# Input projection of a hybrid decoder layer: the weight's hi part times both parts of normed x in one 512-column product, halves summed afterwards

## The chip, the cores and the metric

The kernel runs on one core of a Trainium2 chip. The metric is the device time of one execution in microseconds; lower is better. Each time is the median of repeated executions.

## The reference, cut to what matters

One layer of a decoder with 256 tokens (SEQ), 1024 channels (D_MODEL), float32 throughout:

```python
h = rmsnorm(x, norm_mix)
proj = h @ w_in                                # 1024 x 9488, split into the pieces below
m_z, m_xbc, m_dt, b_qkv, c_qkv, c_f, d_q, d_kv, gate_logits = split(proj)
y_a = mamba2_branch(m_z, m_xbc, m_dt, ...)     # conv of 4 taps, SSD scan, silu(z) gate
y_b = moba_attention(bq, bk, bv, rel_bias)     # with 256 tokens: plain causal attention with bias
y_c = forgetting_attention(cq, ck, cv, c_f)    # bias from a cumulative log forget gate
y_d = sliding_window_attention(dq, dk, dv, sinks, rel_bias)
branch_out = einsum('bsiw,iwd->bsid', stack([y_a, y_b, y_c, y_d]), w_branch)
x = x + sum(sigmoid(gates) * branch_out) @ w_out
h = rmsnorm(x, norm_ffn)
x = x + (silu(h @ w_gate) * (h @ w_up)) @ w_down
out = rmsnorm(x, norm_final)
```

## The kernel before

**Split products.** Every weight and every activation that goes into a large product is cut into a hi part (rounded to the matmul's format fp32r by a copy on ACT) and a lo part (the difference, by DVE). A product is then hi times hi, hi times lo and lo times hi, all added in PSUM. `xx(k)` holds both parts of x for the k-th block of 128 channels as [128, 2, 256]: x times its norm weight, but not yet times the row factor `r1` (the reciprocal root of the mean square), which is applied after the product.

**Weights.** Weights come from HBM in pieces of 1 MB, one after the other in the order of `stream()`: first the projection pieces of `FIRST`, then for each branch its gate pieces and its `wb` pieces, then `wo`, 22 `gu` pieces and 11 `dn` pieces. `fetch` (L333 to L339) issues the load on SP's queue into one of 3 `raw` buffers, `split_hi` (L347) makes the hi part on ACT and `split_lo` (L355) the lo part on DVE, in two halves of 1024 columns each. When the second lo half of a piece is written, the load of the piece three places on is issued.

**Projection pieces.** A transposed piece (all of `xbc`, `z`, `qk` and `qD`; 256 weight columns, the weight is the stationary operand) is computed by `tr_groups` (L493) in two groups j, one for each 128 columns. Both groups share one PSUM bank of the tag `acc` (3 banks). A group of `two` and `mm` is: for each of 8 blocks k the hi weight times x hi (L264) and the hi weight times x lo (L265), 256 columns each, then 8 times the lo weight times x hi (L262). That makes 24 matmuls of 256 columns. A `v` piece and a gate piece (L1044) are natural: x is stationary, the weight moves, 12 matmuls of 512 columns in a group.

**After a product.** One DVE operation over both groups takes the bank out and applies the row factor, broadcast over partitions in `rb` (L936 for q and k, L630 for the convolution's input, L661 for z). `end_v` (L944) and `end_gate` (L968) do it on ACT with a scale for each token.

**Order of the work.** Everything is emitted in one program order; each engine takes its instructions in that order. Between PE's groups the `Weaver` emits the other work. It keeps a planned clock for PE, DVE and ACT. `tick`, called after each group with a cost of 2620 ns (`GROUP`), first runs one step of every urgent task (the ends of products, added by `add`), then lets `split_ahead` cut further weights, then runs steps of the other tasks, each only if DVE's and ACT's planned clocks stay within `SLACK` (3500 ns) of PE's and the buffers it names are free. Buffers are counted by tag: `acc` 3 (PSUM banks), `w2` 6, `w1` 4. `until` runs tasks until given flags are set, whatever the clocks say; `until_free` does the same when a new bank is wanted and none is free.

**The beginning.** x comes transposed with the first weights (`hd`, 8 loads); then `raw_n0`, x again in natural order (`xn`, for the mean square), `raw_qkB0`, small constants, `raw_vB0`, masks and `raw_vB1` follow on SP's queue. PE computes xbc0, n0, a transposed row of `r1` (L477), qkB0, vB0 and vB1, then xbc2 and the other pieces of `FIRST`. The steps of `conv` (SSD's input convolution of xbc0 and xbc1, 2 `w2` buffers each) and `softplus_cums` (a long chain on POOL that gives `dt` and the cumulative sums) run beside them.

**The feed-forward part** already has the form that the change brings: from the fifth `gu` piece on (`wide`, L267, with `normed_x2`, L1157) the hi weight times [x hi | x lo] is one matmul of 512 columns (L273), followed by the lo weight times x hi with 256 columns (L277), and `end_ffn` adds the halves (L1180 on ACT, L1181 on DVE).

**The end.** For each half t of the tokens the last `dn` products are added to the residual (L1265), squared and summed (L1268 on ACT, L1276 on DVE), the reciprocal root is taken on POOL (L1279), the first 512 channels are multiplied by the norm weight (L1280) and scaled on ACT (L1282), the other 512 on DVE (L1283), and the output is stored. In the second half the last 128 channels have a bank of their own, `pd_end`, finished last.

## Time and profile before

| what | value |
|---|---|
| median of 3 runs | 511.25 us (510.37 to 513.1) |
| profiled execution, whole time | 511.43 us |
| profiled execution, span from first to last instruction | 509.7 us |
| mean granted TensorE clock | 0.998 of full speed |
| instructions | 7927 |

The span is what the rows below are measured in, from its start; 1.73 us of the profiled execution lie around it. Busy time of an engine is the time in which it executes; a matmul's own duration is longer than the distance to the next one, since matmuls overlap, so distances between starts are read for PE.

### The profile page before, as it was taken

What the parts mean: (1) busy time and instruction counts of PE and PEld (TensorE: products, weight loads), DVE (VectorE), ACT (ScalarE), POOL (GpSimd) and SP (SyncE); (2) the same over time, 40 slices, a digit from 0 to 9 for tenths busy, and PEclk for the clock granted to TensorE, in tenths of its full rate; (3) what the DMA queues carried; (4) which work ended last, traced back from release to release, by engine and by line L of the source; (5) the groups of instructions that cost most, each with busy time, mean ns of one, the idle gap of its engine ahead of it and who ended that gap; (6) DMA issues with size and microseconds to landing.
All of it is one profiled execution on the core that took longest, in us unless ns stands there. A gap on an engine that the chain in (4) does not pass through costs nothing.

```text
span 509.7 us, 7927 instructions
## 1 busy us (share of the span) xinstructions
PE 501.6 (98%) x3106; PEld 443.5 (87%) x3106; DVE 352.2 (69%) x654; ACT 285.6 (56%) x507; POOL 31.4 (6%) x58
## 2 busy tenths in 40 slices
PE   8999999999999999999999999999999999999994
PEld 8988999979988878788888899998888888888884
DVE  5597689697884969496393676688767767754425
ACT  6687356557465747645535435776556656734322
POOL 0008110011220100000000000000000000000001
PEclk9999999999999999999999999999999999999999
DMA  8964546545455464247266391536456455676202
GB/s 306 386 258 176 201 151 213 211 181 180 167 195 178 131 242 157 114 143 271 82 239 256 101 345 59 196 143 233 166 187 222 168 174 210 237 267 228 84 0 82
DMA packets 16161, 96.06 MB, mean 188 GB/s; under 512 B 1979, under 2 KB 2651, under 8 KB 5884
## 3 DMA queue, kind: packets, MB, share of 16 engines
q1 hardware_dynamic: 14844, 91.36, 49.6%
q0 software_dynamic: 1280, 4.20, 2.7%
q8 instruction: 24, 0.39, 0.3%
q14 instruction: 13, 0.11, 0.1%
HBM read 94.46 MB, written 1.09 MB: 187 GB/s over the span
## 4 chain that ended last, share of the span: by engine, by line
PE 96%; issue 1%; DMA 1%; DVE 0%; ACT 0%; POOLq 0%; POOL 0%; SPq 0%
PE pg L1044 17%; PE gu L273 13%; PE pd L1238 11%; PE pb L262 9%; PE gu L277 7%; PE pvC L1044 2%; PE pvB L1044 2%; PE xbc L451 2%; PE qkC L264 2%; PE qkB L262 2%; PE po L262 2%; PE gu L262 2%; PE qkC L262 2%; PE gu L265 2%; PE qkB L265 2%; PE qkC L265 2%
## 5 line engine op out<-in xcount | busy, mean ns | idle before, releaser
L273 PE MATMUL gu<-x3x,hi_gu 128*128 128x512 f32 x288 | 68.7, 391 | 0.0
L1044 PE MATMUL pg<-hi_g,xx 128*128 128x512 f32 x256 | 64.4, 393 | 0.0
L273 PEld LDWEIGHTS gu<-x3x,hi_gu 128*128 128x128 f32 x288 | 52.9, 188 | 10.3
L355 DVE TENSOR_TENSOR lo_gu<-raw_gu,hi_gu 128x1024 fp32r<-128x1024 f32 x44 | 53.3, 1222 | 6.2 <-ACT hi_gu L347 6.2
L1044 PEld LDWEIGHTS pg<-hi_g,xx 128*128 128x128 f32 x256 | 47.4, 188 | 11.0 <-issue 1.5
L1238 PE MATMUL pd<-hi_dn,aa 128*128 128x512 f32 (+1 forms) x176 | 46.6, 387 | 0.0
L347 ACT ACTIVATE hi_g<-raw_g 128x1024 fp32r<-128x1024 f32 x32 | 32.9, 1053 | 23.8 <-DMA raw_g<-in_w_dram 11.0
L347 ACT ACTIVATE hi_gu<-raw_gu 128x1024 fp32r<-128x1024 f32 x44 | 44.0, 1048 | 1.6 <-PE gu L265 1.6
L355 DVE TENSOR_TENSOR lo_dn<-raw_dn,hi_dn 128x1024 fp32r<-128x1024 f32 x22 | 26.1, 1221 | 21.9 <-ACT hi_dn L347 21.8
L355 DVE TENSOR_TENSOR lo_g<-raw_g,hi_g 128x1024 fp32r<-128x1024 f32 x32 | 38.7, 1234 | 2.7 <-ACT hi_g L347 2.7
L1238 PEld LDWEIGHTS pd<-hi_dn,aa 128*128 128x128 f32 x176 | 32.9, 188 | 6.6
L277 PEld LDWEIGHTS gu<-x3x,lo_gu 128*128 128x128 f32 x288 | 36.9, 191 | 1.4
L277 PE MATMUL gu<-x3x,lo_gu 128*128 128x256 f32 x288 | 37.4, 283 | 0.0
L347 ACT ACTIVATE hi_dn<-raw_dn 128x1024 fp32r<-128x1024 f32 x22 | 22.2, 1051 | 25.2 <-PE pd L1238 25.2
L1044 PE MATMUL pg<-lo_g,xx 128*128 128x512 f32 x128 | 34.2, 389 | 0.0
L1181 DVE TENSOR_TENSOR gs<-gu,ge 128x256 f32<-128x256 f32 x36 | 15.2, 424 | 20.0 <-ACT ge L1180 20.0
L1044 PEld LDWEIGHTS pg<-lo_g,xx 128*128 128x128 f32 x128 | 24.0, 188 | 5.0
L1180 ACT ACTIVATE ge<-gu 128x256 f32<-128x256 f32 x36 | 13.8, 383 | 25.5 <-PE gu L277 25.5
L1238 PE MATMUL pd<-lo_dn,aa 128*128 128x512 f32 (+1 forms) x88 | 26.9, 387 | 0.0
L355 DVE TENSOR_TENSOR lo_wb<-raw_wb,hi_wb 128x1024 fp32r<-128x1024 f32 x16 | 19.4, 1220 | 7.4 <-ACT hi_wb L347 7.4
L968 ACT ACTIVATE gate<-pg,r1h 128x512 f32<-128x512 f32 x16 | 11.0, 688 | 19.9 <-PE pg L1044 19.8
L347 ACT ACTIVATE hi_wb<-raw_wb 128x1024 fp32r<-128x1024 f32 x16 | 16.7, 1055 | 7.3 <-PE pg L1044 7.3
(322 smaller groups left out, 1115.7 us busy)
## 6 DMA issues: line engine op xcount, KB each, us to landing
raw_gu<-in_w_dram SPq DMA_DIRECT2D x22, 1024.0 KB, 4.9
raw_g<-in_w_dram SPq DMA_DIRECT2D x16, 1024.0 KB, 4.9
raw_dn<-in_w_dram SPq DMA_DIRECT2D x11, 1024.0 KB, 4.8
raw_wb<-in_w_dram SPq DMA_DIRECT2D x8, 1024.0 KB, 5.3
raw_qkB<-in_w_dram SPq DMA_DIRECT2D x4, 1024.0 KB, 4.9
raw_qkC<-in_w_dram SPq DMA_DIRECT2D x4, 1024.0 KB, 4.8
raw_wo<-in_w_dram SPq DMA_DIRECT2D x4, 1024.0 KB, 4.8
hd<-in_head_dram SPq DMA_DIRECT2D x7, 384.0 KB, 7.1
```

Of the source, the lines that this page charges most:

```text
L262: pe.matmul(o, l, r, start=start, stop=stop)
L264: pe.matmul(o, l, r[:, 0, :], start=start, stop=False)
L265: pe.matmul(o, l, r[:, 1, :], start=False, stop=stop)
L273: pe.matmul(b, wh(k), x(k), start=i == 0, stop=False)
L277: pe.matmul(b[:, 0, :], wl(k), x(k)[:, 0, :], start=False, stop=i == n - 1)
L347: act.activation(parts[name][0][:, s], raws[name][:, s], AF.Copy)
L355: dve.tensor_tensor(lo[:, s], raws[name][:, s], hi[:, s].bitcast(F32), ALU.subtract)
L968: act.activation(gates[b, t][:, 512 * nh : 512 * nh + 512], p, AF.Tanh, scale=r1h[:, t : t + 1])
L1044: pe.matmul(pg[t], l, r, start=kh == 0 and i == 0, stop=kh == 1 and i == len(terms) - 1)
L1180: act.activation(e[:, j, :], p[j][:, 1, :], AF.Copy)
L1181: dve.tensor_tensor(s[:, j, :], p[j][:, 0, :], e[:, j, :], ALU.add)
L1238: pe.matmul(o, l, r, start=start and j == 0, stop=stop and j == len(terms) - 1)
```

## The change

The pieces from xbc2 on that are not `v` pieces (`WIDE`, 13 pieces of two groups) are computed from a normed x. After the row factor is known, eight tasks `normed_x` make `xr(k)`: x (loaded once more, transposed, as `xTa`) times norm weight times row factor on DVE, a copy to the hi part on ACT, the difference to the lo part on DVE. The stream waits for all eight before xbc2. Each group of a `WIDE` piece has its own bank: 8 matmuls of the hi weight times [x hi | x lo], 512 columns wide, then 8 of the lo weight times x hi into the first 256 columns. `halves` takes the second half of the bank out on ACT and adds it to the first on DVE; for q and for z a constant factor is applied there. The natural pieces after xbc2 (vC and all gates) use `xr` as well, so that their ends scale by a constant. At the end of the kernel the multiplication by the final norm weight moves from the last step of each token half to its first, and the residual addition of the bank whose last 128 columns end later is cut in two.

```diff
--- before.py
+++ after.py
@@ -26,6 +26,11 @@
 
 
 FIRST = ("xbc0 n0 qkB0 vB0 vB1 xbc2 qkB1 xbc3 z0 qkB2 z1 qkB3 qD0 qkC0 vC0 vC1 qkC1 qD1 qkC2 qkC3").split()
+NORMED = FIRST[FIRST.index("xbc2") :]
+WIDE = [n for n in NORMED if n[0] != "v"]
 
 
 
@@ -476,6 +481,35 @@
         for t in range(2):
             pe.transpose(p[:, t, :], r[:, t : t + 1].broadcast_to([128, 128]), ident)
         return flat(p)
+    xa = [slot("xTa%d" % i) for i in range(2)]
+    for i in range(2):
+        nc.sync.dma_start(xa[i], A["xT"][:, 4 * i : 4 * i + 4, :])
+    xr = []
+    def normed_x(k):
+        yield Need(dve=400, act=310, w1=1)
+        if not xr:
+            xr.append(parts_of([slot("xr%d" % i, (128, 2, 2, 256), F32R) for i in range(4)]))
+        u = work("xu%d" % k, [128, 256], "w1")
+        dve.scalar_tensor_tensor(u, xa[k // 4][:, k % 4, :], nm_mix[:, k : k + 1], rb[:, 1, :], ALU.mult, ALU.mult)
+        h_, l_ = (xr[0](k)[:, i, :] for i in range(2))
+        act.activation(h_, u, AF.Copy)
+        yield Need(dve=340)
+        dve.tensor_tensor(l_, u, h_.bitcast(F32), ALU.subtract)
+        rel(w1=1)
+        wv.done.add("xr%d" % k)
+    def halves(o, p, f=1.0):
+        e = work("he", [128, 256], "w1")
+        act.activation(e, p[:, 1, :], AF.Copy, scale=f)
+        if f == 1.0:
+            dve.tensor_tensor(o, p[:, 0, :], e, ALU.add)
+        else:
+            dve.scalar_tensor_tensor(o, p[:, 0, :], f, e, ALU.mult, ALU.add)
+        rel(acc=1, w1=1)
 
 
     def nat_groups(name, hi, lo, n=256):
@@ -623,13 +657,22 @@
 
     def conv(i, p):
 
-        yield Need(dve=650, w2=2)
-        u = work("cu%d" % i, [128, 2, 259], "w2")
-        dve.memset(u[:, :, 0:3], 0.0)
         if i > 1:
-            dve.tensor_tensor(u[:, :, 3:259], p, rb2(1), ALU.mult)
-            rel(acc=1)
+            yield Need(dve=340, act=310, w2=2, w1=1)
+            hold(w2=1)
+            u = work("cu%d" % i, [128, 2, 259], "w2")
+            dve.memset(u[:, :, 0:3], 0.0)
+            for j in range(2):
+                if j:
+                    yield Need(dve=340, act=310, w1=1)
+                while len(p) <= j:
+                    yield Need()
+                halves(u[:, j, 3:259], p[j])
+            rel(w2=1)
         else:
+            yield Need(dve=650, w2=2)
+            u = work("cu%d" % i, [128, 2, 259], "w2")
+            dve.memset(u[:, :, 0:3], 0.0)
             for j in range(2):
                 dve.tensor_tensor(u[:, j, 3:259], p[j], rb[:, 1, :], ALU.mult)
             rel(**{("att", "acc")[i]: 2})
@@ -656,10 +699,17 @@
         wv.done.add("xbc%d" % i)
 
     def silu_z(i, p):
-        yield Need(dve=600, act=520, w2=2)
+        yield Need(dve=340, act=310, w2=2, w1=1)
+        hold(w2=1)
         zh = work("zh%d" % i, [128, 2, 256], "w2")
-        dve.tensor_tensor(zh, p, rb2(2), ALU.mult)
-        rel(acc=1)
+        for j in range(2):
+            if j:
+                yield Need(dve=340, act=310, w1=1)
+            while len(p) <= j:
+                yield Need()
+            halves(zh[:, j, :], p[j], 0.5)
+        rel(w2=1)
+        yield Need(dve=600, act=520, w2=1)
         th = work("zt%d" % i, [128, 2, 256], "w2")
         act.activation(th, zh, AF.Tanh)
         yield Need(dve=600)
@@ -931,6 +981,14 @@
         wv.later(lambda js=js: fox_quad(js), ["qkC%d" % j for j in js] + ["vC0", "vC1", "cum"], True)
 
 
+    def end_halves(name, o, p, fs):
+        for j in range(2):
+            yield Need(dve=340, act=310, w1=1)
+            while len(p) <= j:
+                yield Need(w1=1)
+            halves(o[:, j, :], p[j], fs[j])
+        wv.done.add(name)
     def end_scaled(name, o, p, r):
         yield Need(dve=600)
         dve.tensor_tensor(o, p, r, ALU.mult)
@@ -941,7 +999,7 @@
         yield Need(act=620)
         if br not in v:
             v[br] = slot("v" + br, (128, 2, 512))
-        act.activation(v[br][:, t, :], p, AF.Copy, scale=r1[:, t : t + 1])
+        act.activation(v[br][:, t, :], p, AF.Copy, scale=r1[:, t : t + 1] if "v%s1" % br not in NORMED else 1.0)
         rel(acc=1)
         wv.done.add("v%s%d" % (br, t))
 
@@ -955,17 +1013,18 @@
             br = name[2]
             if i % 2 == 0:
                 qk[br, i // 2] = slot(name)
-            return end_scaled(name, qk[br, i // 2][:, 2 * (i % 2) : 2 * (i % 2) + 2, :], p, rb[:, 0:2, :])
+            o = qk[br, i // 2][:, 2 * (i % 2) : 2 * (i % 2) + 2, :]
+            return end_halves(name, o, p, (0.125, 1.0)) if name in WIDE else end_scaled(name, o, p, rb[:, 0:2, :])
         if name[:2] == "qD":
             if i == 0:
                 qD.append(slot("qD"))
-            return end_scaled(name, qD[0][:, 2 * i : 2 * i + 2, :], p, rb2(0))
+            return end_halves(name, qD[0][:, 2 * i : 2 * i + 2, :], p, (0.125, 0.125))
 
     def end_gate(b, nh, t, p):
         yield Need(act=570)
         if nh == 0:
             gates[b, t] = slot("gate%d%d" % (b, t), (128, 1024))
-        act.activation(gates[b, t][:, 512 * nh : 512 * nh + 512], p, AF.Tanh, scale=r1h[:, t : t + 1])
+        act.activation(gates[b, t][:, 512 * nh : 512 * nh + 512], p, AF.Tanh, scale=0.5)
         rel(acc=1)
 
 
@@ -1013,9 +1072,9 @@
             rel(att=1)
         wv.done.add("mt%d" % nh)
 
-    rb = const("rb", [128, 3, 256])
+    rb = const("rb", [128, 2, 256])
     pg = {}
-    r1n, r1h = const("r1n", [128, 2]), const("r1h", [128, 2])
+    r1n = const("r1n", [128, 2])
     for name in names[1 : names.index("wo00")]:
         if name[:2] == "wb":
             b, nh = int(name[2]), int(name[3])
@@ -1035,11 +1094,12 @@
             b, nh, kh = (int(c) for c in name[1:]) if name[0] == "g" else (name[1], 0, int(name[2]))
             hi, lo = take(name)
             hb, lb = cut(hi, 4, 512), cut(lo, 4, 512)
+            xs_ = xx if names.index(name) < names.index(WIDE[0]) else xr[0]
             for t in (1, 0) if kh else (0, 1):
                 if kh == 0:
                     pg[t] = acc("p%s%d" % (name[:-1], t))
                 terms = three((lambda k: hb[:, k, :], lambda k: lb[:, k, :]),
-                              lambda k: xx(4 * kh + k)[:, :, tok(t)], range(4))
+                              lambda k: xs_(4 * kh + k)[:, :, tok(t)], range(4))
                 for i, (l, r) in enumerate(terms):
                     pe.matmul(pg[t], l, r, start=kh == 0 and i == 0, stop=kh == 1 and i == len(terms) - 1)
                 wv.tick(GROUP)
@@ -1047,7 +1107,23 @@
                     wv.add(end_gate(b, nh, t, pg[t]) if name[0] == "g" else end_v(b, t, pg[t]))
             continue
         first = name == "n0"
+        if name == WIDE[0]:
+            wv.until(["xr%d" % k for k in range(8)])
         hi, lo = take(name)
+        if name in WIDE:
+            hb, lb = cut(hi, 8, 256), cut(lo, 8, 256)
+            p = []
+            for j in range(2):
+                bank = acc(name, [128, 2, 256])
+                for k in range(8):
+                    pe.matmul(bank, hb[:, k, tok(j)], xr[0](k), start=k == 0, stop=False)
+                for k in range(8):
+                    pe.matmul(bank[:, 0, :], lb[:, k, tok(j)], xr[0](k)[:, 0, :], start=False, stop=k == 7)
+                wv.tick(GROUP)
+                p.append(bank)
+                if j == 0:
+                    wv.add(end_of(name, p))
+            continue
         n = sizes[name] // 8
         for p in (nat_groups(name, hi, lo, n) if name[0] == "n" else
                   tr_groups(name, hi, lo, n)):
@@ -1061,14 +1137,15 @@
             r1 = rms("r1", ss1, 1024)
             split_next(0, 2, 2)
             dve.tensor_scalar(r1n, r1, -1.0, None, ALU.mult)
-            dve.tensor_scalar(r1h, r1, 0.5, None, ALU.mult)
             dve.tensor_scalar(tapsh, taps, 0.5, None, ALU.mult)
             dve.tensor_scalar(nsink, sink, -1.0, None, ALU.mult)
             prow = rms_row("r1", r1)
             split_next(1, 2, 2)
-            for i, f in enumerate((1.0, 0.125, 0.5)):
-                act.activation(rb[:, (1, 0, 2)[i], :], prow, AF.Copy, scale=f)
+            for i, f in enumerate((1.0, 0.125)):
+                act.activation(rb[:, 1 - i, :], prow, AF.Copy, scale=f)
             rel(att=1)
+            for k in range(8):
+                wv.tasks.append(Task(normed_x(k)))
         if name != "n0":
             wv.add(end_of(name, p))
 
@@ -1262,11 +1339,15 @@
                 down(c, t, c0, n, bank[:, :n], c == 9 and c0 == 896, c == 10)
             junk = work("sq3_%d%d" % (t, i), [128, 512], "w2")
             e = c0 + bank.shape[-1]
-            dve.tensor_tensor(y[:, c0:e], bank, y[:, c0:e], ALU.add)
+            dve.tensor_tensor(y[:, ns], bank[:, :n], y[:, ns], ALU.add)
             if i < last:
                 ss = const("ss3_%d%d" % (t, i), [128, 1])
                 act.activation(junk[:, :n], y[:, ns], AF.Square, scale=1.0 / 32.0, accum_out=ss)
                 sss.append(ss)
+            if c0 + n < e:
+                dve.tensor_tensor(y[:, c0 + n : e], bank[:, n:], y[:, c0 + n : e], ALU.add)
+            if i == 0:
+                dve.tensor_tensor(o[:, 0:512], y[:, 0:512], nm_fin[:, 0:512], ALU.mult)
             if i == last or i == 0 and last == 2:
                 ms_ = const("ms3_%d%d" % (t, i), [128, 1])
                 dve.tensor_scalar(ms_, sss.pop(), ms, None, ALU.add)
@@ -1277,9 +1358,8 @@
                                          op0=ALU.mult, op1=ALU.add, accum_out=m)
                 r3 = const("r3_%d" % t, [128, 1])
                 pool.tensor_tensor(r3, m, mhalf[:, 0:1], ALU.pow)
-                dve.tensor_tensor(y[:, 0:512], y[:, 0:512], nm_fin[:, 0:512], ALU.mult)
             rel(w2=1)
-        act.activation(o[:, 0:512], y[:, 0:512], AF.Copy, scale=r3)
+        act.activation(o[:, 0:512], o[:, 0:512], AF.Copy, scale=r3)
         dve.scalar_tensor_tensor(o[:, 512:1024], y[:, 512:1024], r3, nm_fin[:, 512:1024], ALU.mult, ALU.mult)
         for h in range(2):
             a, e = 512 * h, 512 * h + 512
```

## Rows read from the trace of the kernel before

**Rows 1.** The page, busy time of each engine, its share of the span, instructions.
```profile
PE 501.6 (98%) x3106; PEld 443.5 (87%) x3106; DVE 352.2 (69%) x654; ACT 285.6 (56%) x507; POOL 31.4 (6%) x58
```

**Rows 2.** The page, the chain that ended last, share of the span by engine.
```profile
PE 96%; issue 1%; DMA 1%; DVE 0%; ACT 0%; POOLq 0%; POOL 0%; SPq 0%
```

**Rows 3.** The chain in order of time: start us, length us, engine and line.
```profile
61.45 0.65 PE sB L794 x8
...
130.88 0.96 PE qkC L262 x8
133.76 0.96 PE qkC L262 x8
...
171.76 8.16 PE pb L262 x36
...
342.38 3.65 PE gu L273 x16
...
442.58 54.44 PE pd L1238 x240
```

**Rows 4.** Groups by line and shape: engine, shapes, xcount | busy us, mean ns | idle before.
```profile
L1181 DVE TENSOR_TENSOR gs<-gu,ge 128x256 f32<-128x256 f32 x36 | 15.2, 424 | 20.0 <-ACT ge L1180 20.0
L1163 DVE SCALAR_TENSOR_TENSOR x<-x2T,chan,rb2b 128x256 f32<-128x256 f32 x8 | 3.4, 478 | 0.0
L1167 DVE TENSOR_TENSOR x3x<-x,x3x 128x256 fp32r<-128x256 f32 x8 | 2.9, 419 | 0.0
L936 DVE TENSOR_TENSOR qkB<-qkB,rb 128x512 f32<-128x512 f32 x4 | 2.8, 689 | 4.6 <-PE qkB L262 4.4
L1180 ACT ACTIVATE ge<-gu 128x256 f32<-128x256 f32 x36 | 13.8, 383 | 25.5 <-PE gu L277 25.5
L1165 ACT ACTIVATE x3x<-x 128x256 fp32r<-128x256 f32 x8 | 3.1, 414 | 1.9 <-DVE x L1163 1.9
```

**Rows 5.** Windows: stretch, its length, busy us (xinstructions) by engine, granted clock, DMA share, GB/s.
```profile
24.00:40.80 16.80, 16.80 (x99) 14.67 (x97) 14.71 (x29) 13.21 (x22) 3.11 (x5) 1.00 0.66 241
40.80:56.00 15.20, 15.20 (x123) 14.41 (x123) 8.32 (x15) 9.52 (x14) 10.83 (x26) 1.00 0.57 218
56.00:76.00 20.00, 20.00 (x171) 19.46 (x171) 16.42 (x48) 10.01 (x27) 1.64 (x3) 1.00 0.46 159
```

**Rows 6.** Windows again, just ahead of the landing of vB1.
```profile
24.00:28.00 4.00, 4.00 (x36) 4.00 (x35) 2.04 (x5) 2.91 (x6) 0.00 (x0) 1.00 1.01 373
```

**Rows 7.** The tile raw_vB: issue on SP's queue, the wait for it, issue to landing.
```profile
20.76 0.33 SPq L339 DMA_DIRECT2D raw_vB<-in_w_dram  x1
...
27.91 2.01 ACT L347 ACTIVATE hi_vB<-raw_vB 128x1024 fp32r<-128x1024 f32 x2 [0.80 <-DMA raw_vB<-in_w_dram]
...
DMA to landing us min/median/max: 7.1/9.5/11.9
```

**Rows 8.** Timeline around the start of xbc2: ACT's and DVE's steps, PE's arrival.
```profile
29.83 1.08 ACT L646 ACTIVATE cc<-cu,tapsh 128x256 f32<-128x256 f32 x2
...
40.84 0.81 PE L516 MATMUL e<-oneh,tab 33*8 33x384 f32 x4
...
42.43 1.27 DVE L355 TENSOR_TENSOR lo_qkB<-raw_qkB,hi_qkB 128x1024 fp32r<-128x1024 f32 x1
```

**Rows 9.** Timeline, POOL's chain to dt: its first step, its first load after it.
```profile
34.33 0.56 POOL L543 TENSOR_SCALAR sp_d<-sp_e 128x32 f32<-128x32 f32 x1 [13.56 <-ACT ea L541]
...
51.45 1.71 POOL L597 DMA_DIRECT2D bB<-erow  x2
```

**Rows 10.** Timeline of the end, DVE and POOL, and the same POOL operation earlier.
```profile
322.46 0.71 POOL L1117 TENSOR_TENSOR r<-r_ms,mhalf 128x2 f32<-128x2 f32 x1 [130.91 <-DVE r_ms L1115]
...
503.88 0.69 DVE L1280 TENSOR_TENSOR x2n<-x2n,nm_fin 128x512 f32<-128x512 f32 x1
504.04 0.94 POOL L1279 TENSOR_TENSOR r<-m,mhalf 128x1 f32<-128x1 f32 x1 [4.44 <-DVE m L1276]
505.01 0.75 DVE L1283 SCALAR_TENSOR_TENSOR out<-x2n,r,nm_fin 128x512 f32<-128x512 f32 x1 [0.45 <-POOL r L1279]
```

## The prediction

> **What bounds the kernel now.** The first view is the page's busy time by engine: PE is busy for 501.6 of 509.7 us, DVE for 352.2, ACT for 285.6 [rows 1]. Busy shares alone don't name the bound, so the chain that ended last comes next: 96% of it is PE, with nearly nothing of DVE or DMA [rows 2]. The chain in order of time shows one PE instruction behind the other from about 24 us to 503 us. So a gap opened in front of a matmul in that stretch is paid in full, and so is every nanosecond taken out of a group. The windows by stage show full PE time at a granted clock of 1.00, that is the 2.4 GHz level, in each stretch read [rows 5]; no stage is slow for its clock. What PE does not pay for now is DVE and ACT: in the first stretch after the row factor, 24 to 40.8 us, they are busy for 14.71 and 13.21 of 16.8 us, and from 40.8 to 56 us for 8.32 and 9.52 of 15.2 [rows 5]. The reader is to see that DVE is nearly full exactly where the change puts new work, and has room just behind it.
>
> The sum is made against the profiled execution, 511.43 us, a span of 509.7 and 1.73 around it. It lies 0.18 us above the median of the runs, 511.25. A change under about 0.5% (2.6 us) can't be told from none here.
>
> **The matmuls.** A group now is 24 matmuls of 256 columns. The chain places the two groups of a qkC piece 133.76 - 130.88 = 2.88 us apart [rows 3], 120 ns a matmul. The new form stands in this trace: the feed-forward part runs 18 pieces of two groups with 8 matmuls of 512 and 8 of 256 columns in each, from 342.38 to 442.58 us, so 100.2 / 36 = 2.783 us a group [rows 3]. Its 16 matmuls of 512 columns take 3.65 us, 228 ns each, against twice 120. The gain is 0.097 us a group, for 13 pieces of 2 groups 26 x 0.097 = 2.5 us. The columns that stream are the same; only a small cost of each matmul is saved. The order differs in one thing: the feed-forward part does both groups' wide matmuls first, the change does group after group. I count that as nothing.
>
> The trace gives 228 ns where 512 columns at 2.4 GHz need 213, and 120 where 256 need 107. The Trainium skill (TensorE: Matmul & The Clock Gate, "Wait — 56ns, not 53.3ns?") says that back-to-back matmuls start N / 2.4 GHz plus about 2.5 ns apart, whatever N is. By that rule the change would save 8 x 2.5 ns a group, an estimate of 0.5 us in all, and speak against the effort. The distances of the trace are 13 to 15 ns above the streaming time, and they decide.
>
> **The new work on DVE and ACT.** The eight steps of normed x have the form of `normed_x2`: 0.478 us and 0.419 us on DVE, 0.414 us on ACT [rows 4], so 7.2 us of DVE and 3.3 of ACT. The ends of products become, for each group, a copy of 0.383 us on ACT and an addition of 0.424 us on DVE [rows 4], against one DVE operation of 0.689 us for a piece. That is 26 x 0.383 = 10.0 us of ACT and 13 x (0.848 - 0.689) = 2.1 us of DVE over some 100 us. ACT stands idle for 5.7 us of the 15.2 after 40.8 us and for 10 us of the next 20 [rows 5], so this is hidden, as long as it comes in time (below). If the cover were gone, these 12 us would not all be paid, since PE waits only for the last.
>
> **Normed x must be there when PE reaches xbc2.** PE arrives at 40.8 us [rows 8], and now also has no bias product to do there, since `bias_rows` waits for dt, which comes later. It needs block k at 40.8 + 0.228 k, the eighth at 42.4. What stands ahead of it: two loads of 512 KB are issued on SP's queue ahead of `raw_vB1`, which is now issued at 20.76 us and lands 7.1 us later, with ACT waiting for it [rows 7]. The DMA engines are full just then, 373 GB/s [rows 6]. 1.05 MB at that rate are 2.8 us, so vB1 lands at about 30.7. Read from the program order, ACT then does the two hi copies of vB1 (2.0), three copies of normed x (1.2), one hi copy of xbc2 (1.0), the four first taps of the convolutions (2 x 1.08 [rows 8]), the other hi copy (1.0) and the fourth normed copy (0.4): 38.5. On DVE follow the difference of block 3, three products, the second lo half of xbc2 (1.27 [rows 8]), three differences, and product, copy and difference of block 7: 0.4 + 1.4 + 1.3 + 1.3 + 0.5 + 0.4 + 0.4 = 5.7, so 44.2. With full durations block 7 is 1.8 us late. Instructions of one engine overlap by some 0.08 us each (two hi copies take 2.01 us [rows 7]), which for about 20 in this chain gives 1.6 us back. Bounds: 0 and 1.8, and 5 if the loads land like the slower of the two raw_vB pieces (11.9 us instead of 7.1 [rows 7]). I take 0.8. Behind it on DVE stand the taps of the convolutions and the lo parts of qkB1; these have the room after 44 us.
>
> **PSUM banks.** Each group has its own bank, so a bank must be empty two groups (5.6 us) after its group ended, before two pieces. The end of a product is an urgent step, emitted one tick later, so three banks suffice if nothing blocks it. Reading the planned clocks by hand, something does: with DVE some 7 us more loaded before xbc2, the last steps of conv 0 and conv 1 don't fit under `SLACK` for several ticks, so they keep 4 of the 6 `w2` buffers; conv 2 (xbc2) takes the other 2, and the end of xbc3, which wants 2, can't start. Its two banks stay taken, and at z0 `until_free` hands out the bank of the group just finished. PE then waits for a copy, an addition and whatever stands before them on ACT and DVE, about 1 us, and once more at the next piece. Bounds: 0 if the conv steps fit earlier, 2 if both waits come whole. I take 1.0.
>
> **The end.** The POOL operation on the last chain takes 0.94 us beside the multiplication L1280, and 0.71 where DVE does nothing beside it [rows 10]. The multiplication goes away from there, so the chain gains 0.2 us; bounds 0 and 0.3. The cut addition adds an instruction of about 0.3 us at a time at which DVE waits for the last bank: nothing.
>
> **The rest at nothing.** One small DVE operation and one copy of the row factor less; the ends of v and gates keep their form, with a constant as scale. dt comes later: POOL's chain takes 51.45 - 34.33 = 17.1 us [rows 9], and its beginning moves behind normed x, about 11 us. The attention that needs it is woven in later; its results are first used by the products of wb at 171.76 us [rows 3], some 100 us after the scores begin.
>
> **Sum.** 511.43 - 2.5 - 0.2 + 0.8 + 1.0 = 510.5 us.
>
> **Rivals.** *No stall at all*, chance 0.25: normed x is in time and the banks are empty, as in the feed-forward part, where eight blocks made the same way just precede the first wide group and PE shows no gap. 511.43 - 2.7 = 508.7, at the edge of what can be told, and down to 508.2 if a group gains a little more. Against it speaks the full DVE before 40.8 us.
>
> *Slower, by late normed x*, chance 0.12: the chain from vB1's landing to block 7 is longer than worked out, and PE stands in front of xbc2. Each us late is a us lost; the gain is used up at 2.7 us, and from 5.3 us the kernel is measurably slower. With vB1 another 4.8 us late the wait is 0.8 + 4.8, so 511.43 - 2.7 + 5.6 + 1.0 = 515.3. For it: ACT takes the hi copies in order and blocks on the landing. Against it: only 1 MB is added.
>
> *Attention rows too late*, chance 0.08: POOL's loads of bias rows come some 11 us after 51.45 [rows 9], while the scores are woven in at 61.45 [rows 3]; DVE waits for the rows with the ends of products behind it, and PE runs out of banks for 3 us: 513.5.
>
> *The wide form gains nothing here*, chance 0.05: the distance of 228 ns holds only when 16 wide matmuls follow each other. Then 511.43 - 0.2 + 1.8 = 513.0. The Trainium skill's fixed cost of 2.5 ns (same page and section) would come near this.
>
> **How the numbers follow.** My forecast, some stall of 1 to 3 us, holds 0.5 of the chance and gives 509.7 to 511.7. The four rivals hold the other 0.5. Faster by over 0.5% (under 508.7): most of the case without a stall, and a little of the forecast, 0.2. Slower (over 513.8): late normed x and half of the late rows, 0.16. The rest, 0.64, is within 0.5%. The range 508.3 to 513.4 leaves out late normed x, half of the late rows and a little of the first rival, 0.2.
>
> **What would show it.** In the profile after: wide groups of a WIDE piece 2.78 us apart; PE idle in front of the first matmuls of xbc2, with a DVE difference as the releaser; PE idle of about 1 us at z0's second group and at qkB2, released by an addition of halves; raw_vB1 landing near 30.7; POOL's last operation near 0.7 us. The prediction is wrong if PE shows no idle time after 24 us, if idle time lies elsewhere, or if the groups are not 2.78 us.

## The result and the profile after

The changed kernel takes 515.98 us (median; 514.73 to 517.07), the kernel before 512.3 us beside it on the same chip: ratio 1.0079, 95% interval 1.0062 to 1.0096. It is slower by 0.8%, 5.5 us above the forecast and 2.6 us above the range. The kernel before ran 0.9 us above the 511.43 us that the sum starts from, so the change itself missed its forecast by 4.6 us: -0.9 expected, +3.7 measured. The profiled span is 514.1 us against 509.7.

The shares of the chain that ended last, to set beside [rows 2]: PE fell from 96% to 84%, DMA and DVE came in.

```profile
PE 84%; DMA 6%; DVE 4%; ACT 3%; issue 1%; SPq 0%; POOLq 0%; POOL 0%; DVEq 0%; ACTq 0%
```

Next the list of what PE waited for (us in total, times, longest). These three stand after the start of xbc2; a fourth and fifth, at the program's start, were there before.

```profile
PE z L1119 <- DVE zh L511: 2.5, 1, 2.5
...
PE cum_n L267 <- POOL av L598: 1.1, 1, 1.1
PE xbc L1119 <- DVE xr L500: 0.8, 1, 0.8
```

All three belong to the change. The largest is at z0's second group. The chain in order of time (start, length) names the way to it, and the two later qkC rows give the distance of groups, as in [rows 3]:

```profile
63.83 3.18 DMA erow<-es
67.14 0.43 DVE zh L511
67.61 3.42 PE z L1119 x8
...
134.80 1.84 PE qkC L1119 x8
...
137.59 1.84 PE qkC L1119 x8
```

DVE's timeline of that time, with the idle time before an instruction and its releaser in brackets:

```profile
62.48 1.22 DVE L360 TENSOR_TENSOR lo_qkB<-raw_qkB,hi_qkB 128x1024 fp32r<-128x1024 f32 x1
67.14 0.42 DVE L511 SCALAR_TENSOR_TENSOR zh<-z,he 128x256 f32<-128x256 f32 x1 [3.43 <-DMA erow<-es]
67.48 1.28 DVE L656 SCALAR_TENSOR_TENSOR bc<-cu,cc 128x512 f32<-128x512 f32 x2
68.68 0.18 DVE L605 COPY cumn<-cum_n 128x32 f32<-128x32 f32 x1
68.79 0.41 DVE L509 TENSOR_TENSOR cu<-xbc,he 128x256 f32<-128x256 f32 x1
```

and ACT's:

```profile
63.34 0.97 ACT L554 ACTIVATE es<-e 8x384 f32<-8x384 f32 x2
64.33 0.39 ACT L507 ACTIVATE he<-z 128x256 f32<-128x256 f32 x1
```

The copy `he` was done at 64.72 us. The addition of z0's halves writes into `zh`, a buffer of the ring `w2`, and it waited for the DMA that stores the attention rows `es`, of the same ring, to `erow` (issued 63.83, done 67.01): the buffer it got was one of theirs (moving them to another ring ends this wait, below). So DVE stood still for 3.43 us, and the bank that PE was to use for z0's second group stayed taken. The last steps of the first two convolutions (`bc`) and the end of xbc3 (`cu<-xbc`) come only after it: the planner did keep back what the prediction said it would.

The store is small, two of 12 KB, and still takes 3.18 us. A load of 1 MB had been issued 1.8 us ahead of it on the same queue:

```profile
62.02 0.33 SPq L344 DMA_DIRECT2D raw_qkB<-in_w_dram  x1
```

By the trace this load landed at 66.81 us, the store at 67.01, and the DMA engines were full in between (64 to 66 us below). In the five other traces in which the store stands in the chain it also ends within 0.5 us of the landing of such a load. No run issues the store ahead of the load, so this reason for its length is not tested.

Behind the two gaps, with 1.3 us of small products between them, PE runs slowly. Windows: stretch, length, busy us (xinstructions) of PE, PEld, DVE, ACT, POOL, granted clock, DMA share, GB/s.

```profile
64.00:66.00 2.00, 1.13 (x10) 0.90 (x9) 0.00 (x0) 1.91 (x4) 0.00 (x0) 1.00 1.01 425
66.00:68.00 2.00, 0.39 (x1) 0.39 (x2) 0.86 (x2) 0.00 (x0) 0.70 (x1) 0.77 0.08 30
68.00:70.00 2.00, 2.00 (x6) 1.52 (x6) 2.00 (x6) 0.00 (x0) 1.00 (x2) 0.50 0.42 104
70.00:72.00 2.00, 2.00 (x13) 1.82 (x12) 0.34 (x1) 0.00 (x0) 0.00 (x0) 0.88 0.70 211
```

A granted clock of 0.50 is the 1.2 GHz level. Z0's eight wide products take 3.42 us in place of 1.84: 1.6 us more.

At xbc2, and at the end:

```profile
42.80 0.43 DVE L500 TENSOR_TENSOR xr<-xu,xr 128x256 fp32r<-128x256 f32 x1 [0.48 <-ACT xr L498]
```
```profile
43.28 0.50 PE L1119 MATMUL xbc<-xr,hi_xbc 128*128 128x512 f32 x1 [0.81 <-DVE xr L500]
```
```profile
508.95 0.55 POOL L1360 TENSOR_TENSOR r<-m,mhalf 128x1 f32<-128x1 f32 x1 [4.83 <-DVE m L1357]
```

**What the terms come to.** 26 groups x (2.88 - 2.79) = -2.3 us; the end -0.4 (POOL's operation 0.55 us, 0.94 in [rows 10]); xbc2 +0.8; cum_n +1.1; z0's second group +2.5 and the slow clock behind it +1.6. Together +3.3 us, where the medians differ by 3.7, the ratio gives 4.0 and the spans differ by 4.4. The list counts idle time. Read as distances between starts, less the usual distance, the three stops are 1.1, 1.2 and 2.6 us, 0.6 more in all. By the same reading the products of the gates and of wb take 133.0 us in place of 132.3, for a reason that no run shows.

### The profile page after: what moved, and what is told of

Read it like the earlier page. It is cut to its first block, busy times and chain, and to the rows that moved or that the text cites. A ratio compares the mean times of both kernels' runs of the same rounds, so it can differ in the third digit from the quotient of the medians.

```text
span 514.1 us, 7563 instructions
## 1 busy us (share of the span) xinstructions
PE 501.9 (98%) x2898; PEld 433.2 (84%) x2898; DVE 359.6 (70%) x683; ACT 292.8 (57%) x540; POOL 29.3 (6%) x58
## 4 chain that ended last, share of the span: by engine, by line
PE 84%; DMA 6%; DVE 4%; ACT 3%; issue 1%; SPq 0%; POOLq 0%; POOL 0%; DVEq 0%; ACTq 0%
PE pg L1104 17%; PE gu L278 13%; PE pd L1315 11%; PE pb L267 9%; PE gu L282 7%; PE qkC L1119 3%; DMA raw_qkB<-in_w_dram 2%; PE pvC L1104 2%; DMA raw_vB<-in_w_dram 2%; PE qkC L1121 2%; PE po L267 1%; PE gu L267 1%; PE po L270 1%; PE gu L270 1%; PE gu L269 1%; PE po L269 1%
## 5 line engine op out<-in xcount | busy, mean ns | idle before, releaser
L1104 PE MATMUL pg<-hi_g,xr 128*128 128x512 f32 x256 | 64.4, 394 | 0.0
L1104 PEld LDWEIGHTS pg<-hi_g,xr 128*128 128x128 f32 x256 | 47.3, 188 | 11.1 <-issue 1.7
L1104 PE MATMUL pg<-lo_g,xr 128*128 128x512 f32 x128 | 34.2, 389 | 0.0
L1104 PEld LDWEIGHTS pg<-lo_g,xr 128*128 128x128 f32 x128 | 24.0, 188 | 5.0
L1027 ACT ACTIVATE gate<-pg 128x512 f32<-128x512 f32 x16 | 9.5, 594 | 18.7 <-PE pg L1104 18.7
```

Of the source, the lines that this page charges most:

```text
L1104: pe.matmul(pg[t], l, r, start=kh == 0 and i == 0, stop=kh == 1 and i == len(terms) - 1)
```

## Experiments

Each ratio is to runs of the kernel before on the same chip, with its 95% interval; "us" is ratio minus one times 511.5.

**The attention rows out of the shared ring.** The tile comes from another ring; the planner's counts stay, so the order of all instructions is the same.

```
-            es = work("es%d" % i, [8, 384], "w2")
+            wv.free["w2"] -= 1
+            es = wk.tile([8, 384], F32, tag="sp", name="es%d" % i, bufs=BUFS["sp"])
```

> The changed kernel, with the two bias-row buffers es taken from another tag than the halves of z0 (the plan's counts are kept, so the order of the work is the same). Theory A, the loss at z0 is one buffer: DVE's addition of z0's first halves waits 3.4 us for the store of es to finish reading, so the bank is late by 2.5 us and PE then runs at the lower clock level for 4 us. Expected: DVE's wait there gone, PE's idle time before z0's second group under 0.6 us, granted clock 1.00 from 66 to 72 us, time 3.5 to 4.2 us below the changed kernel, near 512.0. Theory B, DVE is overfull from the normed blocks on and any wait would come anyway: PE's idle time there stays over 1.5 us and the time falls by less than 1.5 us.

512.5 us, ratio 1.0015 [1.0003, 1.0026]: 3.3 us less than the changed kernel by the ratios, theory A and a little under its 3.5 to 4.2. DVE's addition no longer waits for the store, and the clock stays at 1.00:

```profile
64.11 0.42 DVE L511 SCALAR_TENSOR_TENSOR zh<-z,he 128x256 f32<-128x256 f32 x1 [1.00 <-ACT he L507]
```
```profile
66.00:68.00 2.00, 2.00 (x15) 1.82 (x14) 1.31 (x2) 0.30 (x2) 1.31 (x2) 1.00 0.00 0
```

The store's read of that buffer, with the clock, is most of the slowdown. PE still waits 1.2 us for cum_n and 0.4 for normed x.

**The same edit in the kernel before,** a control.

> The kernel before with its attention rows in buffers of their own, a control. Theory A (in the order of before no addition takes over a buffer that the rows' store still reads, and z0's ends are not asked for a bank between its groups): same as before, ratio 0.999 to 1.001. Theory B (the store's wait on a shared buffer costs the old kernel something too, so that moving the rows is a gain by itself and not a mending of the change): 0.3 % faster or more, and the gain of the changed kernel from the same edit is partly this.

Ratio 0.9994 [0.9980, 1.0008], theory A. The shared buffer cost the old order nothing that can be told; it is the change that brought the store and an urgent addition together.

**The wide form from z0 on only,** xbc2, qkB1 and xbc3 as before.

```
-NORMED = FIRST[FIRST.index("xbc2") :]
+NORMED = FIRST[FIRST.index("z0") :]
```

> The changed kernel, with the wide form and the normed x beginning at z0 and not at xbc2: xbc2, qkB1 and xbc3 keep the old form with one bank a piece, 10 wide pieces are left. Theory A (waits at single places): no idle PE time in front of xbc2 (0.8 us less) and xbc3's banks are not kept; the es buffer may still be in the way of z0. Three pieces of two groups less gain 6 x 0.08 = 0.5 us less. Expected 511 to 513. Theory B (DVE overfull by the normed blocks): these are the same, only their deadline is 17 us later, so this would be at least 3 us below the changed kernel and have no idle PE time after 24 us.

A miss of both theories: 543.84 us, ratio 1.0628 [1.0612, 1.0643]. What PE waited for, and POOL's loads of the ssd rows:

```profile
PE ptC L906 <- DVE pC L895: 11.4, 2, 5.7
PE ya L752 <- DVE dw L787: 3.2, 2, 1.7
```
```profile
87.86 1.11 POOL L631 DMA_DIRECT2D ac<-cumrow  x2 [23.48 <-DMA cumrow<-cum_ts]
186.62 0.54 POOL L631 DMA_DIRECT2D ac<-cumrow  x1 [2.38 <-DVE f L960]
195.78 0.54 POOL L631 DMA_DIRECT2D ac<-cumrow  x1 [8.62 <-DVE f L960]
```

In the kernel before, the last of these loads stands at 91.67 us. Here the second ssd quad was planned behind the other attention quads, to 186 us and later, and PE waits on DVE in that stretch. That the late rows cause these waits is not tested. The run tells nothing about the wide form; it shows how much can come with a small shift of the planned order.

**The new end alone**, put into the kernel before.

> The kernel before with the reordered end alone. The profiles show the last POOL operation at 0.55 us in place of 0.94 us. If that is the end's whole effect: 0.4 us below the kernel before, 0.1%, hardly told from none. A rival, that the end's order costs something by the cut addition: 0 to 0.3 us above.

511.14 against 511.57 us, ratio 0.9989 [0.9975, 1.0003]: in line with 0.4 us, but not told from no change.

**The wide form alone**, with the old end.

> The changed kernel with the end of the kernel before. If the end gives 0.4 us: 0.4 us above the changed kernel, so 4 us above the kernel before. The idle PE times at xbc2 (0.8 us), before the cumulative sums (1.1) and before z0's second group (2.5) and the low clock behind it should stand there unchanged.

516.83 us, ratio 1.0095 [1.0073, 1.0117], 0.8 us above the changed kernel by the ratios where 0.4 was expected, within the noise, and with nearly the same waits on PE. The slowdown is not from the end.

**The wide form taken out, all else kept.** On the kernel with the rows moved, each group as 24 products of 256 columns into the same two halves of its bank; normed x, the ends and the order are the same.

```
-                    pe.matmul(bank, hb[:, k, tok(j)], xr[0](k), start=k == 0, stop=False)
+                    pe.matmul(bank[:, 0, :], hb[:, k, tok(j)], xr[0](k)[:, 0, :], start=k == 0, stop=False)
...
+                for k in range(8):
+                    pe.matmul(bank[:, 1, :], hb[:, k, tok(j)], xr[0](k)[:, 1, :], start=k == 0, stop=k == 7)
```

> The kernel with the attention rows in their own buffers, where each wide group (8 products of 512 columns and 8 of 256) is made of 24 products of 256 columns on the same two halves of the bank, in the same order of everything else, with the same ends. It measures the wide form alone. Theory A (the group saves what the traces show, 2.88 against 2.79 to 2.80 us): 26 times 0.085, 2.2 us slower than the kernel with wide groups, so about 514.7 where the kernel before takes 511.6, ratio 1.006. Theory B (the wide form gains nothing where the halves' additions and normed x hold TensorE anyway): within 0.5 us of the wide kernel, ratio 1.001 to 1.002.

515.1 us, ratio 1.0072 [1.0060, 1.0084]: 2.9 us slower than its pair with wide groups. Theory A, with 2.9 in place of 2.2: the wide form gains what the traces show, and normed x with its ends, without it, makes the kernel 3.7 us slower than before.

**cum_n planned later** (behind z0 and qkB2), once with the rows left in the shared ring and once with them moved.

```
         wv.done.add("dt")
+        wv.later(lambda: cums(av), ["at_qkB2"])
+
+    def cums(av):
         yield Need(pe=650, att=1)
         p1 = att("cum_n", [128, 2, 16])
```

> The changed kernel with cum_n planned behind z0 and qkB2, the attention rows left in the shared buffers. It takes one of the two gaps at z0 away and leaves the other. Theory A (gap and clock are two prices: the 2.5 us wait for the store stays, and TensorE's clock falls behind it as before): 1.1 us faster than the changed kernel, 1.005 to 1.006 of the kernel before, granted clock under 0.9 between 66 and 72 us. Theory B (the clock fell only because the two gaps stood 2 us apart): 2.5 to 3 us faster than the changed kernel, ratio 1.002 to 1.003, granted clock 0.95 or more over 66 to 72 us. Theory C (the store's wait moves with cum_n: the time that TensorE loses less in front of z0's first group it loses more behind it): within 0.5 us of the changed kernel.

> The changed kernel with the attention rows in their own buffers, as in the run before, and with the cumulative-sum product cum_n planned behind z0 and qkB2 instead of between z0's two groups. Theory A (the 1.2 us that TensorE waits there for POOL's softplus chain is a plain wait, and cumrow is not needed soon): TensorE has no listed wait before cum_n and the time falls by 1.2 us against the kernel with the rows alone moved, to the time of the kernel before within 0.3 us (ratio 0.998 to 1.001). Theory B (the wait only moves: the later cum_n makes the ssd rows, or another buffer, late): the time stays within 0.4 us of that kernel, ratio 1.001 to 1.003, with a new wait of 0.8 us or more on TensorE's list.

Rows left: 517.31 us, ratio 1.0110 [1.0092, 1.0128]; rows moved: 512.93, ratio 1.0035 [1.0022, 1.0048]. Both slower than without the edit. Without cum_n in front of it, z0's second group waits 4.3 us and 1.9 us:

```profile
PE z L1123 <- DVE zh L512: 4.3, 1, 4.3
```
```profile
PE z L1124 <- DVE zh L512: 1.9, 1, 1.9
```

So cum_n's 1.1 us was not a price of its own: it covered a part of the wait for the bank, which is 1.9 us without the store and 4.3 with it. For the second kernel this is theory B. For the first it is theory C by its mechanism, the wait moves behind, but not by its size: the kernel is 1.6 us slower than the changed one by the ratios, where C allowed 0.5. Its clock falls to the lower level and stays there longer than in the changed kernel (the trace is of an execution of 519.04 us, the longest of its four); behind the 1.9 us of the second it stays at 1.00 in every window read. The first four lines are the kernel with the rows left, the fifth is the one with the rows moved.

```profile
66.00:68.00 2.00, 0.00 (x0) 0.00 (x0) 0.16 (x1) 0.67 (x1) 0.00 (x0) 0.90 0.49 201
68.00:70.00 2.00, 1.68 (x4) 1.39 (x5) 2.00 (x6) 0.00 (x0) 1.70 (x2) 0.50 0.09 33
70.00:72.00 2.00, 2.00 (x6) 1.52 (x6) 0.95 (x1) 0.00 (x0) 0.00 (x0) 0.50 0.77 234
72.00:74.00 2.00, 2.00 (x10) 1.94 (x9) 0.00 (x0) 0.15 (x1) 0.00 (x0) 0.50 0.86 303
...
64.00:66.00 2.00, 1.82 (x8) 1.51 (x9) 2.00 (x6) 0.90 (x1) 0.00 (x0) 1.00 0.59 246
```

**Another bank for z0's second group**, from the attention pool, in three kernels: alone, with the rows moved, and with rows and cum_n moved.

```
-                bank = acc(name, [128, 2, 256])
+                bank = (att if name == "z0" and j else acc)(name, [128, 2, 256])
```

> The changed kernel with z0's second group in a bank of the attention pool, the attention rows left in the shared buffers. Theory A (TensorE lost its 2.5 us because the bank for this group could not be handed out before the addition that stood behind the rows' store; with a bank at hand the store is not waited for): the 2.5 us are gone, cum_n's 1.1 us stay, the clock stays up, 3 to 4 us faster than the changed kernel, ratio 1.000 to 1.003. Theory B (DVE stands still behind the store for 3.4 us all the same, and the low weights of qkB2, or the next bank, are late by as much): TensorE waits 1.5 us or more at z0's end or qkB2 and the time is at most 1.5 us below the changed kernel, ratio 1.005 or more.

> The changed kernel with the attention rows in their own buffers and z0's second group in a bank of the attention pool (which is free there) instead of one of the three accumulator banks. cum_n stands in front of that group in the order, as before the move. Theory A (the stall at z0 is a wait for the bank that the change takes once more per piece; cum_n's wait for the softplus chain covers it): cum_n still waits 1.0 to 1.5 us, nothing else at z0, and the time is that of the kernel with the rows moved alone, ratio 1.000 to 1.003. Theory B (forcing the waiting tasks in order to free the bank is what made av and the low weights late): no wait over 0.5 us at z0, 1.2 us faster, ratio 0.997 to 0.999.

> All three: the attention rows in their own buffers, z0's second group in a bank of the attention pool, and cum_n planned in front of z1. Theory A (the bank and cum_n are the whole of the stall at z0; each alone only hands it to the other): no listed wait on TensorE between xbc2 and the attention scores over 0.5 us, 1.2 us faster than with the rows moved alone and 1.9 us faster than with rows and cum_n moved, ratio 0.996 to 0.999: just faster than the kernel before. Theory B (the wait goes on to the next bank, at qkB2): ratio 1.000 to 1.003 with a wait of 1 us or more there. The sum of the wide form's gain would then not be had in this order at all.

Alone: 514.25 us, ratio 1.0054 [1.0041, 1.0066]. The time is theory B's, the place is not. PE's wait at z0's second group is gone and the clock is 0.998, but DVE still stands behind the store for 3.4 us, and PE pays some of it at branch B's scores:

```profile
67.30 0.42 DVE L511 SCALAR_TENSOR_TENSOR zh<-z,he 128x256 f32<-128x256 f32 x1 [3.38 <-DMA erow<-es]
```
```profile
PE cum_n L267 <- POOL av L598: 1.1, 1, 1.1
...
PE sB L844 <- DVE xc L739: 0.9, 1, 0.9
```

With the rows moved: 512.6 us, 1.0024 [1.0011, 1.0038], cum_n's 1.1 us the only wait at z0, as theory A had it; moving the rows is thus worth 1.5 us even with a bank at hand. All three: 511.54 us, 1.0000 [0.9990, 1.0010], 4.0 us less than the changed kernel by the ratios. Theory A had the places right, not the time: it expected a kernel just faster than the one before. Nothing is left at z0; what PE still waits for behind the start of xbc2 is

```profile
PE xbc L1124 <- DVE xr L501: 0.7, 1, 0.7
...
PE sB L849 <- DVE xc L744: 0.5, 1, 0.5
PE ptD L907 <- DVE pD L896: 0.2, 1, 0.2
```

**The wide form taken out of that kernel.**

> The run with rows, bank and cum_n moved, with each wide group made of 24 products of 256 columns on the same halves, as in the earlier run of that kind, where z0 still stalled. Theory A (the wide form saves 0.085 us a group wherever no wait hides it): 26 times 0.085, 2.2 us slower than with wide groups, ratio 1.004 to 1.005. Theory B (part of the 2.9 us between the earlier pair came from other waits of the slower stream): 1.5 us or less.

516.13 us, ratio 1.0096 [1.0080, 1.0112]: 4.9 us slower than with wide groups by the ratios, 4.6 by the spans, more than either theory. The distance of the groups gives 2.3 us; the rest comes with more waits for ACT and DVE (the longest below). Behind the start of xbc2 the list sums to 3.0 us, the pair's to 1.4; as distances between starts the stops come to 4.1 and 2.1 us, so little of the 4.6 stays unplaced.

```profile
PE xbc L1124 <- ACT xr L499: 0.9, 1, 0.9
PE qD L1126 <- DVE lo_qD L360: 0.8, 1, 0.8
PE gu L278 <- DVE x3x L1251: 0.5, 1, 0.5
...
PE z L1126 <- DVE lo_z L360: 0.4, 1, 0.4
```

**Normed x earlier**, two ways. First, on the kernel with the rows moved and cum_n late (from z0 on), normed x and the softplus steps as urgent tasks; then, on the kernel with rows, bank and cum_n moved (cum_n from xbc3 on), only vB1's split one piece later (`ahead` 1 while qkB0 runs), so that ACT is free for normed x while `raw_vB1` is on its way.

> As the run with the rows moved and cum_n planned later, and besides the normed x and the softplus steps issued as urgent, ahead of the ACT copies that wait for raw_vB1's transfer. Theory A (normed x is late because its ACT copies stand behind hi_vB1, which waits 3.8 us for its weights): no wait before xbc2's last product, and 0.4 us less than the kernel with rows and cum_n moved. Theory B (DVE's total work before xbc2 is what is late, so an earlier normed x delays the low weights or conv0): TensorE waits at least as long, for another DVE result, and the time is equal or up to 1.5 us more. A case beyond both: the second ssd quad's rows are loaded later in this order, which costs microseconds in the attention stage.

> As the run with the rows in their own buffers, z0's second group in another bank and cum_n planned late, and besides vB1's high weights are split one piece later, so that ACT copies the first normed x pieces and starts the softplus chain before it stands still for raw_vB1. cum_n is planned from xbc3 on, which keeps the order of the ssd rows. Theory A (what is left of the change's gain in that run is lost at xbc2, where DVE's normed x is 0.7 us late, and at the scores of branch B, 0.5 us): neither wait is left, 1.2 us faster, ratio 0.996 to 0.999. Theory B (DVE's work before xbc2 is the limit: what is issued earlier makes lo_vB1 late instead): a wait of 0.7 us or more in front of vB1 or xbc2 and a ratio of 0.999 to 1.003.

527.36 us, 1.0313 [1.0300, 1.0326], and 520.56 us, 1.0182 [1.0168, 1.0197]. Both have theory B's kind of wait and are far slower than it said; the first is the case beyond both that was named. In the second, xbc2 no longer waits, but vB0 does, and cum_n, made earlier in the order, holds z0:

```profile
PE z L1127 <- DVE cumn L610: 3.5, 1, 3.5
PE pvB L1111 <- DVE qkB L999: 3.1, 1, 3.1
```

What DVE does earlier for xbc2 it does later for vB0 and qkB0's end. But its work is not the whole of that: ahead of the first step of normed x DVE itself stands still for the second load of x,

```profile
26.58 0.48 DVE L497 SCALAR_TENSOR_TENSOR xu<-xTa,chan,rb 128x256 f32<-128x256 f32 x1 [2.22 <-DMA xTa<-in_xT_dram]
```

for 2.22 us here and 2.21 in the first, with vB0's lo part and qkB0's end behind it. With that load issued earlier the result could be another; no run tries it. In the first, pvB waits 4.5 us in the same way, PE waits another 4.3 us for POOL's `sqa`, and the last ssd rows are loaded at 151 us.

## Why the prediction was wrong

**The step that failed: PSUM banks, "I take 1.0", bounds 0 and 2.** Its mechanism was there: the end of xbc3 could not start, z0's own bank was handed out, and PE waited at z0's second group for a copy, an addition and what stood before them. Alone this wait is 1.9 us (rows and cum_n out of the way), inside the bounds. What the step did not ask is what buffer the addition writes. It got one that a DMA was still reading, and the 1.9 became 4.3 us; with cum_n in front of it, the changed kernel shows 1.1 us at cum_n and 2.5 behind it. The second wait, at qkB2, did not come. The clock then took 1.6 us more, a price that stood in no bound. In place of the 1.0 us stand 1.1 + 2.5 + 1.6 = 5.2. Taking the store away gives 3.3 us back, giving PE another bank 1.3 us, and both with cum_n planned later 4.0 us.

**"dt comes later", counted at nothing,** was wrong in a way that cost little by itself: cum_n's 1.1 us hide under the bank's wait, and appear only once that is gone (ratio 1.0024 against 1.0000). POOL's chain began 12.1 us later (46.42 for 34.33), near the 11 forecast. The delay matters through `bias_rows`, which waits for dt. Its product moved from 40.84 us [rows 8] to 50.25, and its copies, with the store behind them, from 43.07 to 63.34. Here are the copies before and the product after:

```profile
43.07 0.97 ACT L520 ACTIVATE es<-e 8x384 f32<-8x384 f32 x2
```
```profile
50.25 0.82 PE L550 MATMUL e<-oneh,tab 33*8 33x384 f32 x4
```

So 9.4 of these 20.3 us stand in front of the product and 10.9 between product and copies. The step of the copies asks the planner for two `w2` buffers, the kind that the end of xbc3 lacked. That this held them up is read from the code and not tested. Both together put the store at the moment at which z0's halves needed the buffer.

**Attention rows too late** (a rival at 0.08) named the right transfer and the right victim, the ends of products, but by a wrong path: not a load of the rows that DVE needs, but a store of them that still holds a buffer.

**Late normed x**: taken as 0.8, measured 0.8, released by the difference of the last block as said. The landing of raw_vB1, worked out as 30.7 us, ended ACT's wait at 31.02:

```profile
31.02 2.01 ACT L352 ACTIVATE hi_vB<-raw_vB 128x1024 fp32r<-128x1024 f32 x2 [4.35 <-DMA raw_vB<-in_w_dram]
```

Two tries to have normed x earlier moved the wait to vB0, with DVE standing still for x's second load in both.

**The matmuls**: 2.79 us a group against 2.783 worked out. The rate is borne out (2.3 us), and taking the wide form out costs 2.9 and 4.9 us in two pairs of kernels, other waits included. Eight matmuls fewer a group save 0.09 us, 11 ns each. By the rule that the prediction cited from the Trainium skill (TensorE: Matmul & The Clock Gate, "Wait — 56ns, not 53.3ns?") it would have been 2.5 ns each; the measured distance decides against it here.

**The end**: -0.2 forecast, POOL's operation now 0.55 us instead of 0.94. The forecast took the 0.71 us of another place as the floor.

**"ACT and DVE are hidden"** is where the gain went once z0 was mended. With wide groups and no wait at z0 the kernel equals the one before. So, by subtraction, normed x and the ends of halves cost what the wide form and the end give, 2.3 + 0.4 = 2.7 us. As distances between starts, PE's stops in that kernel come to 2.1 us of it (1.4 as listed idle time: 0.7, 0.5, 0.2; a fourth, of 0.1 in qD, is too short for the list), and the products of the gates and of wb are 0.6 us longer than before, for a reason that no run shows. The three listed stops are released by steps of DVE, but only the first by a step of normed x; that the other two come from DVE's added work is argued and not tested. No version tried here is faster than the kernel before by more than the noise.

## What to carry to other kernels

When a change moves a step to another time, list the buffers that its transfers hold, and who takes these next: a compute instruction can wait for a store's read just as for a load, and a small store behind a large load may hold its buffer until that load has landed. A wait that PE shows may cover a longer one behind it; take both away before pricing either. And a saving that is real at PE (0.09 us a group) has to be set against the DVE and ACT work that buys it, in the stretch where these engines are fullest.

## What the runs showed that I had not expected

PE's clock fell to the 1.2 GHz level behind idle times of 1.1 and 2.5 us with only 1.3 us of small products between them, and behind one of 4.3 us, and cost 1.6 us in the first case. It stayed up behind 1.9 us and behind 1.2 us.

The same POOL operation on a column of 128 took 0.94 us beside a DVE multiplication [rows 10] and 0.55 us with DVE idle; the runs that part the end from the wide form repeat it, 0.55 us with the new end alone and 0.94 with the old end. The Trainium skill (SBUF — State Buffer, "Who interferes with whom") says that a DVE instruction with two inputs from SBUF contends with a GpSimd instruction that reads SBUF; the two numbers agree with it.
